# Expert blocks of a mixture-of-experts stage that hold at most 64 tokens: both parts of the tokens in one matmul operand

## The chip, the cores and the metric

The kernel runs on one core of a Trainium2 chip. The metric is the device time of one execution in microseconds (us), lower is better. The kernel before took 2165.18 us (median of three runs, 2159.99 to 2166.26).

The engines are named as the profile names them: PE is TensorE, DVE VectorE, ACT ScalarE, POOL GpSimd and SP SyncE. [...]

## What is computed

The reference is one layer: a recurrent token mixer, and then a mixture of experts over 1024 tokens of width 1024. Only the second half of the expert part matters here. Each token goes to 8 of 64 experts. The 8192 assignments are sorted by expert and each expert's list is padded to blocks of 128 rows. Then for each block:

```python
def expert_block(acc, blk):
    toks, wr, e = blk
    xb = x_pad[toks]                                   # 128 rows gathered
    hid = jax.nn.silu(xb @ w1[e]) * (xb @ w3[e])       # "up": 1024 -> 256, twice
    return acc.at[toks].add((hid @ w2[e]) * wr[:, None].astype(xb.dtype)), None   # "down", scattered
```

The reference works in float32.

## The kernel before, in words

**Numbers in two parts.** [...] So each operand is split into a high part, which is the value cast to `F32R`, and a low part, which is the value less its high part. A product is then three matmuls into the same accumulator: high by high, high by low, low by high. The helper `mm3` (L1639 to L1642) issues these three passes; L1640, L1641 and L1642 are its lines.

**Routing.** One function (up to L1537) computes on the chip which expert each block has, which tokens it holds and where they go. VectorE does most of it. It leaves `gi` and `si` (rows to gather and to scatter, one column for each block), `beb` (the expert of each block) and `meta`, a row of integers: 128 experts, 128 flags that say whether a block's expert differs from that of the block two places before (the weights are kept in two sets, for even and odd blocks), and the number of blocks. The blocks are dealt out so that even positions go through the first half of the experts' list and odd positions through the second half. Places of a block without a token gather row 0 and scatter to spare rows.

**The block loop** is `moe` (L1540 on). Its order is written out by hand (`tc.manual_schedule`), each engine takes its instructions in that order, and the function `group` (L1692) holds it. For block b, in order:

- `gather(b + 2)`: POOL gathers 128 rows of the tokens (L1611), two buffers.
- `up(b)`: TensorE multiplies the transposed tokens (stationary, `xh` and `xl`) by the expert's first weights (moving, `wh` and `wl`, 512 columns for both up matrices), eight pieces of the depth with three passes each, into `pa`.
- `hid_split(b - 1)`: ScalarE and VectorE split the hidden values of the block before into `hh` and `hl`.
- `store(b - 2)`: ScalarE scales the result by the token's weight (L1687), POOL scatters it with addition (L1689).
- `split_l(b - 1, 2)`, `split_h(b + 1, 0)`, `split_l(b + 1, 0)`, `split_h(b + 1, 1)`: ScalarE casts a 1 MB piece of weights to its high part (L1598), VectorE takes the difference (L1604). Each expert has three pieces: 0 and 1 for up, 2 for down. They stand under `fresh`, a `tc.If` on the block's flag, so that they run only when the expert is new. After a difference, SP loads the same piece for the block two later (L1581), conditional on that block's flag.
- `act(b)`: Silu on ScalarE (L1655), and its product with the other half on VectorE, `hd` (L1656).
- `x_t(b + 1)`, `x_split(b + 1)`: TensorE transposes the gathered tokens of the next block into `pt` (L1621), ScalarE casts them to `xh` (L1631) and VectorE takes the difference `xl` (L1632), in two halves; a small instruction (L1636, `jk`) picks the token's weight.
- `split_h(b, 2)`, `split_l(b + 1, 1)`: the remaining pieces of weights.
- `down(b - 1)`: twelve matmuls into `py`, and `hid_t(b)`: TensorE transposes `hd` into `ph` (L1663).

`xh` and `xl` have one buffer each, `pa` and the weights two. The first 95 blocks (`NB0`) run always; the rest of the possible 128 stand in groups of three under a `tc.If` on the number of blocks (L1741), and all engines jump over them here. After the loop come the final sum and norm.

When a `tc.If` is not taken, the engine still has to raise its semaphore by what the skipped instructions would have raised. It does so with an event instruction that first waits until the engine's earlier instructions are done.

Of the kernel before, what the change touches and what calls it, by code (L numbers as in the profile page):

```python
# [21 lines left out]
DVE = mybir.EngineType.DVE  # L22

# [7 lines left out]
NB = 128  # L31
NB0 = T * 8 // P + 64 // 2 - 1
# [9 lines left out]
def tile_kernel(ctx: ExitStack, tc: tile.TileContext, A: dict, dbg=None):  # L42
# [919 lines left out]
    meta = rt.tile([1, 2 * NB + 1], I32, name="meta")  # L962
# [410 lines left out]
def dispatch(nc, tc, A, ident, ones, sc, gi, si, beb, iot, meta, h2d):  # L1373
    V, S, G, PE = nc.vector, nc.scalar, nc.gpsimd, nc.tensor
    with tc.tile_pool(name="ds", bufs=1, side="right", reuse_waits="tile") as q, \
# [91 lines left out]
        V.tensor_tensor(pst, pend, nbk, ALU.subtract)  # L1467
        V.tensor_scalar(pst, pst, float(P), 1.0, ALU.mult, ALU.add)
# [38 lines left out]
        pbe = qp.tile([P, NB], F32, name="pbe")  # L1507
        PE.matmul(pbe, ones, dg, start=True, stop=True)
        V.tensor_copy(beb, pbe)
        br_ = beb[0:1]  # L1510
# [8 lines left out]
        V.tensor_copy(meta[:, 2 * NB :], nb[0:1])  # L1519
# [20 lines left out]
def moe(nc, tc, A, ident, h2d, accs, gi, si, beb, iot, meta, later):  # L1540
    V, S, G, PE = nc.vector, nc.scalar, nc.gpsimd, nc.tensor
    with tc.tile_pool(name="mo", bufs=1, reuse_waits="tile") as q, tc.tile_pool(name="mop", bufs=1, space=PSUM, reuse_waits="tile") as qp:
# [41 lines left out]

        def fresh(b, eng):
# [38 lines left out]
        def x_split(b):  # L1624
            if b >= NB:
                return
            xh = rot(q, [P, D], F32R, "xh", 1)
            xl = rot(q, [P, D], F32R, "xl", 1)
            for hf in range(2):
                s = slice(hf * 512, hf * 512 + 512)  # L1630
                S.copy(xh[:, s], PX[b][hf])  # L1631
                V.tensor_tensor(xl[:, s], PX[b][hf], xh[:, s].bitcast(F32), ALU.subtract)  # L1632
            XT[b] = xh, xl

            jk = rot(q, [P, 64], F32, "jk", 2)
            V.scalar_tensor_tensor(jk, iot[:, :64], beb[:, b : b + 1], XG[b][:, D:], ALU.is_equal, ALU.mult,  # L1636
                                   accum_out=rw[:, b : b + 1])

        def mm3(out, lh, ll, rh, rl, start, stop):  # L1639
            PE.matmul(out, lh, rh, start=start, stop=False)  # L1640
            PE.matmul(out, lh, rl, start=False, stop=False)  # L1641
            PE.matmul(out, ll, rh, start=False, stop=stop)  # L1642

        def up(b):
            AA[b] = rot(qp, [P, 512], F32, "pa", 2)
            for k in range(KD):
                ws = slice((k % 4) * 512, (k % 4) * 512 + 512)
                ks = slice(k * P, k * P + P)
                mm3(AA[b], XT[b][0][:, ks], XT[b][1][:, ks], WH[b, k // 4][:, ws], WL[b, k // 4][:, ws],
                    k == 0, k == KD - 1)  # L1650
# [33 lines left out]
        def store(b):  # L1684
            if b in YP:
                y = rot(q, [P, D], F32, "y", 2)
                S.mul(y, YP.pop(b), rw[:, b : b + 1])  # L1687

                G.indirect_dma_start(accs[b % 2], IndirectOffsetOnAxis(ap=si[:, b : b + 1], axis=0), y, None,  # L1689
                                     compute_op=ALU.add)  # L1690

        def group(lo, hi):  # L1692
            split_h(lo, 0)
            split_l(lo, 0)
            x_t(lo)
            x_split(lo)
            split_h(lo, 1)
            split_l(lo, 1)
            for b in range(lo, hi):
# [23 lines left out]
                if b > lo:  # L1723
                    down(b - 1)
# [6 lines left out]
        with tc.manual_schedule():  # L1731
# [7 lines left out]
            nb = nc.values_load(meta[0:1, 2 * NB : 2 * NB + 1], min_val=0, max_val=NB,  # L1739
# [170 lines left out]
```

## Time and profile before

| | us |
|---|---|
| median of three runs | 2165.18 |
| the profiled execution | 2165.25 |
| its span, first to last instruction | 2163.5 |
| expert loop, first up product to last down product | 1184.8 to 2095.1 |
| PE busy | 2040.4 (94%), 10575 matmuls and as many weight loads |
| DVE busy | 1282.8 (59%) |
| ACT busy | 992.4 (46%) |
| POOL busy | 541.7 (25%) |
[...]

The expert loop fills the second half of the span. A matmul's row has a modelled end: the next one starts before it. The distance from start to start is what a matmul costs when nothing waits. "Idle before" is the engine's pause ahead of an instruction, with what ended it. A name with a small q (PEldq, ACTq) is the engine's sequencer: register loads, branches and event instructions, which do not count as busy.

### The profile page before, as it was taken

To read this page: it belongs to the slowest core of one execution; us is meant where nothing else is said; L and a number is where in the kernel's file an instruction comes from. 1 tells how busy PE (TensorE), PEld (TensorE's weight loads), DVE (VectorE), ACT (ScalarE), POOL (GpSimd) and SP (SyncE) were. 2 spreads that over 40 slices of the span, in tenths; PEclk is the share of its full clock that TensorE was granted. 3 is DMA by queue.
4 is the path that set the end of the run, shared out by engine and by line. 5 is a ranking of instruction groups with operands and counts; after the bars stand their busy time and mean duration, and the time that the engine had idled before them with its cause. 6 is when DMAs were issued, how large, how long until landed. Compare 5 with 4: busy or idle time off the path is not lost. (4 is left out here: it accounts for less than half of the span.)

```text
span 2163.5 us, 29638 instructions
## 1 busy us (share of the span) xinstructions
PE 2040.4 (94%) x10575; PEld 1658.1 (77%) x10575; DVE 1282.8 (59%) x2047; ACT 992.4 (46%) x1352; POOL 541.7 (25%) x395
## 2 busy tenths in 40 slices
PE   6799999999999999998999999999989999999983
PEld 2488888898777788876777888788878888787861
DVE  7854664645668543444577666666454657775726
ACT  4335554634533411113234566566454657765721
POOL 5510000000033000010101344444333434444421
PEclk8799999999999999998998999999999999999996
DMA  8250100101053443456435799899898899999969
GB/s 306 73 153 26 40 30 30 39 30 49 30 172 135 142 137 116 128 170 245 159 111 224 248 307 338 258 313 297 240 310 240 267 280 358 368 347 270 332 136 238
DMA packets 107800, 416.17 MB, mean 192 GB/s; under 512 B 15250, under 2 KB 22034, under 8 KB 87668
## 3 DMA queue, kind: packets, MB, share of 16 engines
q1 hardware_dynamic: 62688, 260.03, 34.1%
q0 software_dynamic: 35376, 135.65, 23.6%
q10 hardware_dynamic: 9572, 18.46, 2.4%
q8 instruction: 85, 1.39, 0.3%
q14 instruction: 79, 0.65, 0.1%
HBM read 465.44 MB, written 90.20 MB: 257 GB/s over the span
## 5 line engine op out<-in xcount | busy, mean ns | idle before, releaser
L1604 DVE TENSOR_TENSOR wl<-raw,wh 128x2048 fp32r<-128x2048 f32 x156 | 356.3, 2288 | 61.4 <-ACT wh L1598 61.4
L1598 ACT CAST wh<-raw 128x2048 fp32r<-128x2048 f32 x156 | 294.8, 1919 | 43.0 <-DMA raw<-in_wm_dram 42.9
L1640 PE MATMUL pa<-wh,xh 128*128 128x512 f32 x760 | 304.9, 401 | 0.2 <-ACT xh L1631 0.2
L1641 PE MATMUL pa<-wl,xh 128*128 128x512 f32 x760 | 298.2, 392 | 2.8 <-DVE wl L1604 2.8
L1642 PE MATMUL pa<-wh,xl 128*128 128x512 f32 x760 | 298.7, 393 | 0.1
L1611 POOL DMA_INDIRECT xg<-h2d,gi x97 | 164.3, 1694 | 480.1 <-issue 326.5
L81 PE MATMUL z<-xl,wH 128*128 128x512 f32 x672 | 271.3, 404 | 8.1 <-DVE xl L293 8.1
L80 PE MATMUL z<-hH,wH 128*128 128x512 f32 x672 | 269.2, 401 | 2.7 <-ACT hH L290 1.6
L82 PE MATMUL z<-hH,wL 128*128 128x512 f32 x672 | 267.8, 399 | 0.0
L1689 POOL DMA_INDIRECT acc<-y,si x95 | 214.7, 2261 | 90.1 <-ACT y L1687 47.7
L1641 PEld LDWEIGHTS pa<-wl,xh 128*128 128x128 f32 x760 | 143.5, 189 | 33.6 <-DVE wl L1604 6.5
L1642 PEld LDWEIGHTS pa<-wh,xl 128*128 128x128 f32 x760 | 143.0, 188 | 32.2 <-DVE xl L1632 2.4
L1640 PEld LDWEIGHTS pa<-wh,xh 128*128 128x128 f32 x760 | 143.2, 188 | 27.2 <-ACT xh L1631 0.5
L1640 PE MATMUL py<-wh,hh 128*128 128x512 f32 x380 | 156.8, 413 | 6.4 <-ACT y L1687 6.4
L81 PEld LDWEIGHTS z<-xl,wH 128*128 128x128 f32 x672 | 127.8, 190 | 35.2 <-DVE xl L293 11.8
L1641 PE MATMUL py<-wl,hh 128*128 128x512 f32 x380 | 149.1, 392 | 0.8 <-DVE wl L1604 0.8
L80 PEld LDWEIGHTS z<-hH,wH 128*128 128x128 f32 x672 | 127.7, 190 | 28.1 <-ACT hH L290 1.8
L1642 PE MATMUL py<-wh,hl 128*128 128x512 f32 x380 | 149.1, 392 | 0.0
L82 PEld LDWEIGHTS z<-hH,wL 128*128 128x128 f32 x672 | 128.1, 191 | 24.6 <-issue 0.7
L125 DVE TENSOR_TENSOR wL<-wraw,wH 128x1024 fp32r<-128x1024 f32 x56 | 73.4, 1318 | 121.9 <-ACT wH L120 121.7
L1656 DVE TENSOR_TENSOR hd<-sl,pa 128x256 f32<-128x256 f32 x95 | 40.0, 421 | 175.2 <-ACT sl L1655 175.2
L1632 DVE TENSOR_TENSOR xl<-pt,xh 128x512 fp32r<-128x512 f32 x190 | 122.4, 686 | 18.6 <-ACT xh L1631 18.1
(522 smaller groups left out, 3897.5 us busy)
## 6 DMA issues: line engine op xcount, KB each, us to landing
raw<-in_wm_dram SPq DMA_DIRECT2D x285, 1024.0 KB
wraw<-in_wz_dram SPq DMA_DIRECT2D x50, 512.0 KB
wk<-in_w_ada_dram SPq DMA_DIRECT2D x64, 256.0 KB
raw<-in_wm_dram POOLq DMA_DIRECT2D x6, 1024.0 KB, 7.7
acc<-x POOLq DMA_DIRECT2D x9, 512.0 KB, 5.8
xl<-in_xcT_dram SPq DMA_DIRECT2D x16, 256.0 KB
mgd<-ga POOLq DMA_DIRECT2D x16, 256.0 KB, 3.1
xr<-in_xc_dram SPq DMA_DIRECT2D x8, 512.0 KB
```

The costliest lines, as they stand in the source:

```text
L80: PE.matmul(out, lh, rh, start=start, stop=False)
L81: PE.matmul(out, lh, rl, start=False, stop=False)
L82: return PE.matmul(out, ll, rh, start=False, stop=stop)
L125: V.tensor_tensor(L, raw, H.bitcast(F32), ALU.subtract)
L1598: S.copy(WH[b, c], raw[b % 2][c])
L1604: V.tensor_tensor(WL[b, c], raw[b % 2][c], WH[b, c].bitcast(F32), ALU.subtract)
L1611: G.indirect_dma_start(XG[b], None, h2d, IndirectOffsetOnAxis(ap=gi[:, b : b + 1], axis=0))
L1632: V.tensor_tensor(xl[:, s], PX[b][hf], xh[:, s].bitcast(F32), ALU.subtract)
L1640: PE.matmul(out, lh, rh, start=start, stop=False)
L1641: PE.matmul(out, lh, rl, start=False, stop=False)
L1642: PE.matmul(out, ll, rh, start=False, stop=stop)
L1689: G.indirect_dma_start(accs[b % 2], IndirectOffsetOnAxis(ap=si[:, b : b + 1], axis=0), y, None, compute_op=ALU.add)
```

## The change

For a block with at most 64 tokens, the 128 columns of the stationary operand hold the high parts of 64 tokens and, beside them, the low parts of the same 64 tokens. Two passes, against the weights' high and low parts, then give two sets of rows of `pa`, and their sum is the result; it holds the product low by low too. The routing makes a flag for each block, `half`, which each engine loads into a register and branches on. Such blocks gather and scatter 64 rows. All other parts of a block (transposes, casts, down products) stay at 128 rows.

```diff
-    meta = rt.tile([1, 2 * NB + 1], I32, name="meta")
+    meta = rt.tile([1, 3 * NB + 1], I32, name="meta")
...
+        rend = q.tile([P, 64], F32, name="rend")
+        V.scalar_tensor_tensor(rend, pst, float(P), cnt, ALU.mult, ALU.add)
+        pst0 = q.tile([P, 64], F32, name="pst0")
+        V.tensor_copy(pst0, pst)
...
+        ls = q.tile([P, 64], F32, name="ls")
+        V.tensor_scalar(ls, pst0, pb, None, ALU.is_le)
+        V.tensor_tensor(ls, ls, le, ALU.subtract)
+        V.tensor_tensor(ls, ls, rend, ALU.mult)
+        rem = q.tile([P, 1], F32, name="rem")
+        V.tensor_reduce(rem, ls, AX.X, ALU.add)
+        V.scalar_tensor_tensor(rem, pb, -float(P), rem, ALU.mult, ALU.add)
+        V.tensor_scalar(rem, rem, P / 2 + 0.5, None, ALU.is_lt)
+        dgh = q.tile([P, P], F32, name="dgh", tag="dg")
+        V.tensor_scalar(dgh, ident, rem, None, ALU.mult)
+        PE.matmul(pbh, ones, dgh, start=True, stop=True)
...
+        V.tensor_copy(meta[:, 2 * NB : 3 * NB], pbh[0:1])
...
+        def half(b, eng):
+            if (b, eng, 0) not in flags:
+                flags[b, eng, 0] = nc.values_load(meta[0:1, 2 * NB + b : 2 * NB + b + 1], engines=[eng], ...)
+            return tc.If(flags[b, eng, 0] > 0)
...
             XG[b] = rot(q, [P, D + 64], F32, "xg", 2)
-            G.indirect_dma_start(XG[b], None, h2d, IndirectOffsetOnAxis(ap=gi[:, b : b + 1], axis=0))
+            if b < 2:
+                G.memset(XG[b][H2:], 0.0)
+            with half(b, POOL) as c:
+                G.indirect_dma_start(XG[b][:H2], None, h2d, IndirectOffsetOnAxis(ap=gi[:H2, b : b + 1], axis=0))
+            with c.Else():
+                G.indirect_dma_start(XG[b], None, h2d, IndirectOffsetOnAxis(ap=gi[:, b : b + 1], axis=0))
...
                 S.copy(xh[:, s], PX[b][hf])
-                V.tensor_tensor(xl[:, s], PX[b][hf], xh[:, s].bitcast(F32), ALU.subtract)
+            with half(b, DVE) as c:
+                for hf in range(2):
+                    rest(xh[:, hf * 512 : hf * 512 + 512], PX[b][hf])
+            with c.Else():
+                for hf in range(2):
+                    s = slice(hf * 512, hf * 512 + 512)
+                    V.tensor_tensor(xl[:, s], PX[b][hf], xh[:, s].bitcast(F32), ALU.subtract)
...
+        def rest(h, x):
+            v = h.rearrange("p (k t) -> p k t", t=P)
+            V.tensor_tensor(v[:, :, H2:], x.rearrange("p (k t) -> p k t", t=P)[:, :, :H2],
+                            v[:, :, :H2].bitcast(F32), ALU.subtract)
...
         def mm3(out, lh, ll, rh, rl, start, stop):
             PE.matmul(out, lh, rh, start=start, stop=False)
-            PE.matmul(out, lh, rl, start=False, stop=False)
-            PE.matmul(out, ll, rh, start=False, stop=stop)
+            PE.matmul(out, lh, rl, start=False, stop=stop and ll is None)
+            if ll is not None:
+                PE.matmul(out, ll, rh, start=False, stop=stop)
...
+            def products(xl):
+                for k in range(KD):
+                    ...
+                    mm3(AA[b], XT[b][0][:, ks], XT[b][1][:, ks] if xl else None, WH[b, k // 4][:, ws], WL[b, k // 4][:, ws],
+                        k == 0, k == KD - 1)
+            with half(b, TEN) as c:
+                products(False)
+            with c.Else():
+                products(True)
...
+            tu = rot(q, [H2, 512], F32, "tu", 1)
+            hv = [slice(i * 256, i * 256 + 256) for i in range(2)]
+            with half(b, ACT):
+                for v in hv:
+                    S.copy(tu[:, v], AA[b][H2:, v])
+            with half(b, DVE):
+                for v in hv:
+                    V.tensor_tensor(AA[b][:H2, v], AA[b][:H2, v], tu[:, v], ALU.add)
             S.activation(sl, AA[b][:, :256], AF.Silu)
...
+                with half(b, POOL) as c:
+                    G.indirect_dma_start(accs[b % 2], IndirectOffsetOnAxis(ap=si[:H2, b : b + 1], axis=0), y[:H2], None,
+                                         compute_op=ALU.add)
+                with c.Else():
+                    G.indirect_dma_start(accs[b % 2], IndirectOffsetOnAxis(ap=si[:, b : b + 1], axis=0), y, None,
+                                         compute_op=ALU.add)
```

`H2` is 64. `jk` has one buffer in place of two.

## Rows read from the trace of the kernel before

**Rows 1.** The page's groups: line, engine, operation, names, count | busy us, mean ns | idle.

```profile
L1598 ACT CAST wh<-raw 128x2048 fp32r<-128x2048 f32 x156 | 294.8, 1919 | 43.0 <-DMA raw<-in_wm_dram 42.9
L1642 PE MATMUL pa<-wh,xl 128*128 128x512 f32 x760 | 298.7, 393 | 0.1
L1611 POOL DMA_INDIRECT xg<-h2d,gi x97 | 164.3, 1694 | 480.1 <-issue 326.5
L1689 POOL DMA_INDIRECT acc<-y,si x95 | 214.7, 2261 | 90.1 <-ACT y L1687 47.7
```

**Rows 2.** Busy time by stretch of the expert loop; columns named in the rows.

```profile
core 0: us, PE busy (x) PEld busy (x) DVE busy (x) ACT busy (x) POOL busy (x), PEclk, DMA share, GB/s
...
1290.00:1390.00 100.00, 95.53 (x464) 77.32 (x463) 72.75 (x83) 68.08 (x72) 45.63 (x22) 1.00 0.97 315
1390.00:1490.00 100.00, 100.00 (x498) 83.38 (x496) 55.83 (x80) 55.34 (x67) 38.68 (x22) 1.00 0.93 289
...
sum 910.00, PE 893.77 PEld 738.11 DVE 566.71 ACT 548.57 POOL 373.75; mean PE 89.38 PEld 73.81 DVE 56.67 ACT 54.86 POOL 37.38
```

**Rows 3.** TensorE in order of time, one block: start us, us, what.

```profile
1646.74 0.48 PE L1640 MATMUL pa<-wh,xh 128*128 128x512 f32 x1
...
1652.07 0.39 PE L1642 MATMUL pa<-wh,xl 128*128 128x512 f32 x1
1652.30 1.03 PE L1621 MATMUL pt<-ident,xg 128*128 128x128 f32 x8
...
1656.05 0.48 PE L1640 MATMUL pa<-wh,xh 128*128 128x512 f32 x1
```

**Rows 4.** Instructions of one line (L1597): count, ns min/median/max, first and last start.

```profile
L1597 ACTq EVENT_SEMAPHORE  x129: 17/17/17, 1206.0 to 2083.6; - x129
```

**Rows 5.** The same for line L1640, weight loads and the sequencer.

```profile
L1640 PEld LDWEIGHTS pa<-wh,xh x760: 186/188/331, 1184.8 to 2086.6; 128*128 128x128 f32 x190
...
L1640 PEldq EVENT_SEMAPHORE  x1: 51/51/51, 1184.4 to 1184.4; - x1
```

**Rows 6.** VectorE in order of time, block with a new expert next.

```profile
1668.86 2.29 DVE L1604 TENSOR_TENSOR wl<-raw,wh 128x2048 fp32r<-128x2048 f32 x1 [2.39 <-ACT wh L1598]
1671.53 0.42 DVE L1656 TENSOR_TENSOR hd<-sl,pa 128x256 f32<-128x256 f32 x1 [0.38 <-ACT sl L1655]
1672.17 1.29 DVE L1632 TENSOR_TENSOR xl<-pt,xh 128x512 fp32r<-128x512 f32 x2 [0.22 <-ACT xh L1631]
```

**Rows 7.** TensorE in order of time, start of that block.

```profile
1665.36 0.48 PE L1640 MATMUL pa<-wh,xh 128*128 128x512 f32 x1
```

**Rows 8.** ScalarE in order of time, the same block.

```profile
1666.92 3.72 ACT L1598 CAST wh<-raw 128x2048 fp32r<-128x2048 f32 x2
...
1671.55 1.08 ACT L1631 CAST xh<-pt 128x512 fp32r<-128x512 f32 x2
```

**Rows 9.** Instructions of line L1739, register loads after the loop.

```profile
L1739 PEldq TENSOR_LOAD <-meta x1: 483/483/483, 2092.1 to 2092.1; - x1
```

**Rows 10.** Instructions of line L1741, the branch over unused groups.

```profile
L1741 PEldq COMPARE_BRANCH  x1: 3746/3746/3746, 2092.7 to 2092.7; - x1
...
L1741 POOLq INC_SWDGE_SEM  x1: 1987/1987/1987, 2102.8 to 2102.8; - x1
```

**Rows 11.** TensorE in order of time, the last twelve down products.

```profile
2092.05 0.50 PE L1640 MATMUL py<-wh,hh 128*128 128x512 f32 x1 [1.48 <-ACT y L1687]
...
2094.68 0.39 PE L1642 MATMUL py<-wh,hl 128*128 128x512 f32 x1
```

**Rows 12.** VectorE in order of time, routing.

```profile
1142.60 0.22 DVE L1496 SCALAR_TENSOR_TENSOR bf<-pf,isb 128x64 f32<-128x64 f32 x1
```

**Rows 13.** DMA queues of the page: kind, packets, MB, share of 16 engines.

```profile
q8 instruction: 85, 1.39, 0.3%
q14 instruction: 79, 0.65, 0.1%
```

**Rows 14.** DMA issues by line: count, median us from issue to landing.

```profile
xg<-h2d,gi POOLq DMA_INDIRECT x97, 9.2
...
acc<-y,si POOLq DMA_INDIRECT x95, 11.5
```

More of the change, by code (lines that the diff above doesn't have):

```diff
@@ L22 @@
 DVE = mybir.EngineType.DVE
+TEN = mybir.EngineType.PE
 P = 128
@@ L31 @@
 NB = 128
+H2 = 64
 NB0 = T * 8 // P + 64 // 2 - 1
@@ L1518, in dispatch @@
         V.tensor_copy(meta[:, NB : 2 * NB], fl)
-        V.tensor_copy(meta[:, 2 * NB :], nb[0:1])
+        V.tensor_copy(meta[:, 2 * NB : 3 * NB], pbh[0:1])
+        V.tensor_copy(meta[:, 3 * NB :], nb[0:1])
         pl = qp.tile([P, NB], F32, name="pl")
@@ L1583, in moe @@
         flags = {}
+        def half(b, eng):
+            if (b, eng, 0) not in flags:
+                flags[b, eng, 0] = nc.values_load(meta[0:1, 2 * NB + b : 2 * NB + b + 1], engines=[eng], min_val=0,
+                                                  max_val=1, skip_runtime_bounds_check_because="made on chip within these bounds")
+            return tc.If(flags[b, eng, 0] > 0)
         def fresh(b, eng):
@@ L1631, in x_split @@
                 S.copy(xh[:, s], PX[b][hf])
-                V.tensor_tensor(xl[:, s], PX[b][hf], xh[:, s].bitcast(F32), ALU.subtract)
+            with half(b, DVE) as c:
[5 more added lines that the diff above has]
+                    V.tensor_tensor(xl[:, s], PX[b][hf], xh[:, s].bitcast(F32), ALU.subtract)
             XT[b] = xh, xl
-            jk = rot(q, [P, 64], F32, "jk", 2)
+            jk = rot(q, [P, 64], F32, "jk", 1)
             V.scalar_tensor_tensor(jk, iot[:, :64], beb[:, b : b + 1], XG[b][:, D:], ALU.is_equal, ALU.mult,
                                    accum_out=rw[:, b : b + 1])
+        def rest(h, x):
+            v = h.rearrange("p (k t) -> p k t", t=P)
+            V.tensor_tensor(v[:, :, H2:], x.rearrange("p (k t) -> p k t", t=P)[:, :, :H2],
+                            v[:, :, :H2].bitcast(F32), ALU.subtract)
         def mm3(out, lh, ll, rh, rl, start, stop):
             PE.matmul(out, lh, rh, start=start, stop=False)
-            PE.matmul(out, lh, rl, start=False, stop=False)
-            PE.matmul(out, ll, rh, start=False, stop=stop)
+            PE.matmul(out, lh, rl, start=False, stop=stop and ll is None)
+            if ll is not None:
+                PE.matmul(out, ll, rh, start=False, stop=stop)
         def up(b):
             AA[b] = rot(qp, [P, 512], F32, "pa", 2)
[L1646 to L1650, printed above, removed]
+            def products(xl):
+                for k in range(KD):
+                    ws = slice((k % 4) * 512, (k % 4) * 512 + 512)
+                    ks = slice(k * P, k * P + P)
+                    mm3(AA[b], XT[b][0][:, ks], XT[b][1][:, ks] if xl else None, WH[b, k // 4][:, ws], WL[b, k // 4][:, ws],
[4 more added lines that the diff above has]
+                products(True)
         def act(b):
@@ L1686, in store, with group @@
                 y = rot(q, [P, D], F32, "y", 2)
[L1687 to L1699, printed above, removed]
+                py = YP.pop(b)
+                S.mul(y, py, rw[:, b : b + 1])
+                with half(b, POOL) as c:
[4 more added lines that the diff above has]
+                                         compute_op=ALU.add)
+        def group(first_, hi):
+            split_h(first_, 0)
+            split_l(first_, 0)
+            x_t(first_)
+            x_split(first_)
+            split_h(first_, 1)
+            split_l(first_, 1)
+            for b in range(first_, hi):
                 last = b == hi - 1
@@ L1722, in group @@
                     split_l(b + 1, 1)
-                if b > lo:
+                if b > first_:
                     down(b - 1)
```

5 lines of the change are left out of this document (3 added, 2 removed).

## The prediction

> **What bounds the kernel now.** I read the page's groups first, then the table by stretch, then TensorE's order of time inside a block, then ScalarE and VectorE in the same block. The groups tell how often the loop runs: the up products are 760 of each of three passes, so 95 blocks of eight, and 156 casts `wh<-raw` are 52 experts of three pieces [rows 1]. That fits the reference's routing: worked out from its inputs (default seed), 52 experts get tokens, in 95 blocks, and 33 of the 95 hold at most 64 tokens. The table shows who is the limit: over the 910 us of the expert loop TensorE is busy 893.8, all of 1390 to 1490, and 4.5 us short in 1290 to 1390, where DMA's share is 0.97 and one new expert follows another [rows 2]. [...] So the loop is TensorE's, with small holes where weights come late.
>
> Inside a block nothing waits: up runs from 1646.74 to the transposes at 1652.30, and these, the down products and the hidden transposes lead to the next up at 1656.05 [rows 3]. A block takes 9.31 us; the 24 up products take 5.56 with the slower first one, 0.227 each (the last row of up and the next row are 0.23 apart).
>
> **The change part by part.**
>
> *Eight products fewer.* Eight times 0.227 is 1.81 us for each of 33 blocks: 60 us at most. This is the whole gain on offer; the transposes, the down products and the hidden transposes stay at 128 rows.
>
> *The join of the short arm.* The two arms raise TensorE's semaphore by different amounts, so the short one must add the rest after its own last product is done. ScalarE shows the habit: its skipped casts, three in each of 93 blocks less 150 done (156 without the first two blocks' six), are 129, and there are 129 event instructions [rows 4]. For TensorE the trace has no join between products. From below it costs nothing (the last product's increment could carry the difference). From above: the tail of a product past the next one's start, 0.39 less 0.23, and what lies between an event instruction and the weight load behind it, from 1184.4 to 1184.8 [rows 3, 5], together some 0.55. I take 0.5, by these rows: 1.3 us is left of 1.81.
>
> *The sum of the two parts, and its own chain.* Before Silu, ScalarE now copies two pieces of 64x256 and VectorE adds two. The nearest row is `hd`, as wide, at 0.42 [rows 6]. Two copies that overlap a little take some 0.7 (an estimate; at most 0.84), and the last add ends 0.45 after the last copy: 1.15 us longer to Silu. Whether that matters depends on the next block.
>
> Next block of an old expert (16 blocks, by the routing, and the last block): up ends at +3.7, Silu is done at +5.4, `hd` at +5.9, the two `xl` at about +7.2. TensorE, with join, transposes and down products, wants the next up at 9.31 - 1.81 + 0.5 = 8.0. All is hidden. 17 times 1.3 is 22 us.
>
> Next block of a new expert (16 blocks): ScalarE first casts that expert's first two pieces. In the block that starts at 1665.36 [rows 7] these run 1666.92 to 1670.64, that is to +5.3, and VectorE's `wl` ends at 1671.15, +5.8 [rows 6, 8]. Up at 3.7 is no help there: copies to +6.0, adds to +6.7, Silu +7.1, `xh` (1.08) +8.2, the second `xl` +9.1, and the next up now waits for both `xl`, as either arm of the split may have written `xh`. So the next block starts at +9.1, not +9.31; where it is itself a half block (5 of 16) the two differences of 64 rows are shorter and it is +8.7. That is 11 times 0.2 and 5 times 0.6: 5 us. Bounds: nothing to lose or gain beyond -0.5 each (-8) and 1.3 each (+21).
>
> *Branches.* Each block adds one register load and a branch on TensorE, ScalarE, VectorE and GpSimd. TensorE's one load in the trace took 0.48, its branch came 0.6 after the load's start [rows 9, 10]. The load ran at 2092.11, while the twelve down products of 2092.05 to 2094.68 were still to be done [rows 11]: its sequencer is at least 2.5 us ahead of its array. So I cost it at nothing; after a short arm's join that lead is rebuilt during the down products. Uncovered it would be 0.6 a block. On ScalarE and VectorE the branch and the join of the skipped copies come while they wait for TensorE; nothing in the 62 full blocks, where the later Silu (it waits for VectorE's join, after `wl` at +5.8) still leaves `xl` at +8.5 against 9.31.
>
> *Blocks where weights are late.* The loop's idle is 910 - 893.8 = 16 us [rows 2]. Fewer gathered and scattered rows free DMA there, which gives back nothing to 4.5 us, the hole of 1290 to 1390. But an up that waits for the second `xl` loses 0.65 (half of the pair's 1.29 [rows 6]) in each block that weights hold up, some eight (an estimate: 16 us at about 2 a hole): 5 us. Faster blocks before them also reach late weights sooner. I take -3 us (a loss), bounds -8 and +4.5.
>
> *GpSimd.* Gather and scatter cost it 1.69 + 2.26 = 3.95 us a block [rows 1]; it has 5.3 free. Added are the load and, if each arm's transfer has a semaphore of its own, a correction for the arm not taken. The only such row took 1.99 [rows 10]. Two of them make 8.4 with a load as long as TensorE's: still below 9.31. Nothing, as long as it fits.
>
> *Routing.* Some ten small VectorE instructions like `bf`, 0.22 each (a little over half of that from start to start, estimated, as they overlap) [rows 12], stand in a stretch in which VectorE has no pause: 1.4 us, bounds 0 (the shared expert's products fill TensorE) and 2.2.
>
> *Sum.* 22 + 5 - 3 - 1.4 = 23 us off the profiled execution's 2165.25 (span 2163.5, the rest around it): 2142 us. That execution lies on the median shown, 2165.18.
>
> [...] Short jumps cost no extra code loading in this trace: with 129 skipped casts on ScalarE alone [rows 4], one instruction queue brought 0.65 MB in 79 pages for all its engines; and another's 85 pages of 1.39 MB are TensorE's 21150 instructions once, 66 bytes each [rows 13]. The one long jump kept TensorE's sequencer 3.75 us [rows 10]. [...]
>
> **The rivals.**
> 1. *More is kept*: no join on TensorE, ScalarE's chain shorter than I add it, DMA's relief real. 17 times 1.81, 16 times 0.6, +3: 43 us, 2122. For it: the last product's increment may carry the difference. Against: ScalarE is busy to +5.3 whatever up does.
> 2. *TensorE leaves its queue at each branch*: 0.6 in 62 full blocks and 17 short ones is 47 us, 2142 + 47 = 2189, slower; half of it would be 2166. Against: the load's row with twelve products behind it.
> 3. *GpSimd becomes the loop's bound*: it decides when a correction costs more than (9.31 - 3.95 - 0.48) / 2 = 2.4 us. At 3.0, a wait for an old transfer before each 1.99, a full block takes 10.4, 62 times 1.1 is 68 us, and the half blocks lose their gain against some 8.5 (33 times 0.8 is 26 less): 2165 + 68 - 26 = 2207, slower. For it: transfers take 9.2 and 11.5 us to land [rows 14], and four semaphores a block in place of two come round sooner. Against: a block's room.
> [...]
> 5. *It hardly takes effect* (the flag is set for few blocks, or the gathers wait as before and weights set the pace): 2166, the same.
>
> **How the numbers follow.** Forecast 0.58, its own range 2128 to 2156; rival 1 0.16; 2 0.08, of which half near 2166; 3 0.08; 4 0.04; 5 0.06. What a measurement of this kernel can tell from no change is about 0.3%, 6.5 us. Faster: 0.56 + 0.16, so 0.72; the same: 0.02 of the forecast, 0.06 of rival 5, 0.04 of rival 2, so 0.12; slower 0.16. The range 2116 to 2172 takes in the forecast, most of rival 1, rival 5 and the mild half of rival 2.
>
> **What would show it.** `pa` third pass 496 times, the others 760. TensorE's time from an up's first product to the transposes 5.6 in full blocks, 3.7 plus the join in short ones. Blocks with an old expert behind them at about 8.0, with a new expert at 8.7 to 9.1, full ones at 9.31. Wrong is the prediction if full blocks stretch beyond 9.5 without late weights (rivals 2 to 4: the wait then names TensorE's queue, or `xg`), or if short blocks before a new expert reach 8.0.

## The result, and the profile after

The changed kernel takes 2142.8 us (median of four, 2141.1 to 2144.0) beside 2163.6 for the kernel before: ratio 0.9904, interval [0.9886, 0.9923], some 21 us faster. The profiled execution has a span of 2140.0 us against 2163.5. Forecast were 2142 us and a range of 2116 to 2172.

The page after: the lines that answer to [rows 1] and [rows 13], with the two busiest groups of the loop.

```profile
q0 software_dynamic: 31088, 117.53, 21.2%
...
q8 instruction: 99, 1.62, 0.3%
q14 instruction: 103, 0.84, 0.1%
...
L1633 DVE TENSOR_TENSOR wl<-raw,wh 128x2048 fp32r<-128x2048 f32 x156 | 355.8, 2285 | 42.8 <-ACT wh L1627 39.2
L1686 PE MATMUL pa<-wh,xh 128*128 128x512 f32 x760 | 310.5, 409 | 15.4 <-DVE xl L1672 8.7
L1627 ACT CAST wh<-raw 128x2048 fp32r<-128x2048 f32 x156 | 295.1, 1922 | 26.1 <-DMA raw<-in_wm_dram 25.9
...
L1689 PE MATMUL pa<-wh,xl 128*128 128x512 f32 x496 | 195.8, 395 | 0.0
L1645 POOL DMA_INDIRECT xg<-h2d,gi x63 | 113.9, 1809 | 299.0 <-DVE jk L1676 139.8
...
L1756 POOL DMA_INDIRECT acc<-y,si x62 | 150.7, 2430 | 46.2 <-ACT y L1750 20.5
```

The third pass runs 496 times, 62 blocks of eight, so 33 blocks take the short arm. The first pass of up (L1686) now has 15.4 us of idle time ahead of it, 8.7 of it put down to `xl`. ScalarE waits less for weights than before (25.9 us, 42.9 in [rows 1]).

A short block before an old expert, TensorE in order of time (block 30, the kernel after):

```profile
1466.10 0.48 PE L1686 MATMUL pa<-wh,xh 128*128 128x512 f32 x1
...
1469.61 0.39 PE L1687 MATMUL pa<-wl,xh 128*128 128x512 f32 x1
1469.85 1.03 PE L1655 MATMUL pt<-ident,xg 128*128 128x128 f32 x8
...
1473.46 0.38 PE L1725 MATMUL ph<-ident,hd 128*128 128x128 f32 x2
1473.59 0.48 PE L1686 MATMUL pa<-wh,xh 128*128 128x512 f32 x1
```

7.49 us from up to up, where [rows 3] show 9.31: 1.82 less, which is the eight products. Between the last up product (1469.61) and the transposes there is no wait for a join; in 31 of the 32 short blocks that another block follows the two starts are 0.23 to 0.24 apart.

A short block before a new expert is another matter (block 53, the kernel after; first TensorE, then ScalarE, then VectorE):

```profile
1679.82 0.47 PE L1686 MATMUL pa<-wh,xh 128*128 128x512 f32 x1
...
1683.34 0.39 PE L1687 MATMUL pa<-wl,xh 128*128 128x512 f32 x1
...
1686.95 0.39 PE L1689 MATMUL py<-wh,hl 128*128 128x512 f32 x1
1688.47 0.44 PE L1725 MATMUL ph<-ident,hd 128*128 128x128 f32 x2 [1.13 <-DVE hd L1718]
1689.51 0.47 PE L1686 MATMUL pa<-wh,xh 128*128 128x512 f32 x1 [0.60 <-ACT hh L1731]
```

```profile
1680.87 0.39 ACT L1731 CAST hh<-ph 128x256 fp32r<-128x256 f32 x1
1681.13 1.15 ACT L1750 ACTIVATE y<-py,rw 128x1024 f32<-128x1024 f32 x1
1682.13 3.75 ACT L1627 CAST wh<-raw 128x2048 fp32r<-128x2048 f32 x2
1685.91 0.64 ACT L1713 COPY tu<-pa 64x256 f32<-64x256 f32 x2
1687.58 0.38 ACT L1717 ACTIVATE sl<-pa 128x256 f32<-128x256 f32 x1 [1.03 <-DVE pa L1716]
1687.86 1.07 ACT L1665 CAST xh<-pt 128x512 fp32r<-128x512 f32 x2
```

```profile
1684.11 2.29 DVE L1633 TENSOR_TENSOR wl<-raw,wh 128x2048 fp32r<-128x2048 f32 x1 [0.20 <-ACT wh L1627]
1686.58 0.89 DVE L1716 TENSOR_TENSOR pa<-pa,tu 64x256 f32<-64x256 f32 x2 [0.18 <-ACT tu L1713]
1687.99 0.42 DVE L1718 TENSOR_TENSOR hd<-sl,pa 128x256 f32<-128x256 f32 x1 [0.53 <-ACT sl L1717]
1688.67 1.29 DVE L1672 TENSOR_TENSOR xl<-pt,xh 128x512 fp32r<-128x512 f32 x2 [0.26 <-ACT xh L1665]
```

The up products are done at 1683.6, but ScalarE casts the next expert's pieces until 1685.88, and only then starts the copies of the join. VectorE's `wl` ends at 1686.40, at about the same place. Then copies, additions, Silu, `xh` and `xl` follow one another, and the next up starts 9.69 us after this one. The bracket names `hh`; but what the next up waits for in all 16 such blocks is the first of the two `xl` (0.69 from 1688.67, so 1689.36): TensorE starts 0.14 to 0.26 after its end. In the kernel before the first up product needed no `xl`. In the kernel before the same block reads thus on ScalarE and VectorE:

```profile
1694.84 3.73 ACT L1598 CAST wh<-raw 128x2048 fp32r<-128x2048 f32 x2
1699.03 0.39 ACT L1655 ACTIVATE sl<-pa 128x256 f32<-128x256 f32 x1 [0.47 <-PE pa L1642]
```

It began at 1693.28. Its Silu came 5.75 after the start, that of the kernel after 7.76. The idle time ahead of the earlier Silu is put down to the up products: there ScalarE was done with the copies in time.

By the class of the block, from first up product to first up product, the sums of the two profiled executions are:

| | before | after | difference |
|---|---|---|---|
| up to the first up product | 1184.79 | 1185.22 | +0.4 |
| 16 short blocks, old expert next | 149.53 | 127.95 | -21.6 |
| 16 short blocks, new expert next | 155.19 | 157.08 | +1.9 |
| 62 full blocks | 592.40 | 594.68 | +2.3 |
| from the last block's up (short) to the end | 81.62 | 75.11 | -6.5 |

They add up to the span's 23.5 us. So the blocks before an old expert gave most of what TensorE saved, and those before a new one, taken together, nothing. These 16 fall in two: in the kernel before 12 of them take 9.32 us on the mean, and four, in which the weights of one new expert after another are late (blocks 17, 18, 78 and 79; in the kernel before block 78 still took 9.31), 10.85. After, the 12 take 9.17 and the four 11.77.

### The profile page after: what moved, and what is told of

It reads as the page before. It is cut to its first block, busy times and chain, and to the rows that moved or that the text cites. A ratio compares the mean times of both kernels' runs of the same rounds, so it can differ in the third digit from the quotient of the medians.

```text
span 2140.0 us, 30952 instructions
## 1 busy us (share of the span) xinstructions
PE 1994.5 (93%) x10313; PEld 1609.4 (75%) x10313; DVE 1298.0 (61%) x2123; ACT 1004.7 (47%) x1418; POOL 544.9 (25%) x397
## 5 line engine op out<-in xcount | busy, mean ns | idle before, releaser
L1686 PE MATMUL pa<-wh,xh 128*128 128x512 f32 x760 | 310.5, 409 | 15.4 <-DVE xl L1672 8.7
L1627 ACT CAST wh<-raw 128x2048 fp32r<-128x2048 f32 x156 | 295.1, 1922 | 26.1 <-DMA raw<-in_wm_dram 25.9
L1689 PE MATMUL pa<-wh,xl 128*128 128x512 f32 x496 | 195.8, 395 | 0.0
L1645 POOL DMA_INDIRECT xg<-h2d,gi x63 | 113.9, 1809 | 299.0 <-DVE jk L1676 139.8
L1686 PEld LDWEIGHTS pa<-wh,xh 128*128 128x128 f32 x760 | 146.3, 193 | 50.8 <-ACT xh L1665 7.6
L1756 POOL DMA_INDIRECT acc<-y,si x62 | 150.7, 2430 | 46.2 <-ACT y L1750 20.5
L1686 PE MATMUL py<-wh,hh 128*128 128x512 f32 x380 | 156.9, 413 | 4.6 <-ACT y L1750 4.6
L84 PEld LDWEIGHTS z<-hH,wL 128*128 128x128 f32 x672 | 128.0, 190 | 24.5 <-issue 0.7
L122 ACT CAST wH<-wraw 128x1024 fp32r<-128x1024 f32 x56 | 58.8, 1050 | 148.6 <-PE z L83 66.3
L1717 ACT ACTIVATE sl<-pa 128x256 f32<-128x256 f32 x95 | 36.5, 384 | 180.7 <-PE pa L1689 112.7
```

Source lines behind the costliest of these rows:

```text
L84: return PE.matmul(out, ll, rh, start=False, stop=stop)
L122: S.copy(H, raw)
L1627: S.copy(WH[b, c], raw[b % 2][c])
```

## The experiments

Ratios are to the kernel before on the same chip. Medians of the same kernel differ by several us from one set of executions to another (2159.0 to 2163.6 for the kernel before), so I read the ratios, and inside the loop the traces' starts. These recur: the kernel before and the kernel with branches but no gain (*branch_only*) agree within 0.7 us in each class of the table above, and within 1.4 us in each of the two groups of the new-expert class. Each kernel has one trace. Five of them (old_next, old_split, order, half_load_before, half_wh) are of executions 7 to 10 us below their kernel's median, and part of that lies ahead of the loop: their first up product comes at 1176.4 to 1181.6, that of the others at 1182.4 to 1188.2. So differences of a few us between loops are not shown by two traces alone. Means over the blocks, us after the block's first up product; "12" and "4" are the blocks before a new expert with weights in time and with late ones:

| kernel | ratio | old next: next up | 12: second weight copy ends | 12: Silu starts | 12: next up | 4: next up | first to last up | of it at half the full clock |
|---|---|---|---|---|---|---|---|---|
| before | 1 | 9.35 | 5.29 | 5.97 | 9.32 | 10.85 | 897.1 | 10.2 |
| branch_only | 1.0014 | 9.37 | 5.30 | 6.04 | 9.43 | 10.60 | 897.3 | 6.8 |
| rows_only | 0.9953 | 9.35 | 5.28 | 6.05 | 9.40 | 9.31 | 886.0 | 10.2 |
| up_only | 0.9948 | 7.88 | 5.71 | 7.40 | 9.25 | 12.21 | 882.7 | 30.5 |
| after | 0.9904 | 8.00 | 5.59 | 7.30 | 9.17 | 11.77 | 879.7 | 30.7 |
| old_next | 0.9892 | 7.97 | 5.66 | 6.26 | 9.17 | 11.01 | 872.7 | 10.2 |
| old_split | 0.9882 | 7.99 | 5.34 | 6.16 | 9.29 | 10.68 | 871.2 | 6.5 |
| no_sum | 0.9770 | 7.60 | 5.33 | 5.24 | 7.50 | 11.22 | 849.1 | 20.5 |
| order | 0.9978 | 8.27 | - | 7.59 | 9.50 | 11.48 | 892.0 | 17.1 |
| half_load_before | 0.9944 | 9.35 | 5.28 | 5.97 | 9.32 | 9.31 | 877.7 | 0 |
| half_load | 0.9861 | 7.95 | 5.54 | 7.26 | 9.22 | 10.36 | 871.6 | 17.1 |
| half_wl | 0.9879 | 7.75 | 5.64 | 7.24 | 9.10 | 11.92 | 873.8 | 30.7 |
| half_wh | 0.9865 | 7.87 | 3.72 | 6.37 | 8.24 | 12.10 | 862.4 | 20.5 |

(The copy's mean leaves out block 0, whose copies lie further back; a recorded start can lie a little ahead of the end of the instruction before it, as 5.24 beside 5.33 in *no_sum*.)

**branch_only: the branches without their gain.**

```diff
-                products(False)
+                products(True)
-                    rest(xh[:, hf * 512 : hf * 512 + 512], PX[b][hf])
+                    V.tensor_tensor(xl[:, s], PX[b][hf], xh[:, s].bitcast(F32), ALU.subtract)
-                G.indirect_dma_start(XG[b][:H2], ..., gi[:H2, b : b + 1] ...)
+                G.indirect_dma_start(XG[b], ..., gi[:, b : b + 1] ...)
```

(the scatter likewise; the join is gone, and with it ScalarE's branch and VectorE's second one)

> All the branches of the change on TensorE, VectorE (around the low parts) and GpSimd stay, but both arms do the whole work: 24 products, both low parts full, 128 rows; the sums and ScalarE's branch are left out. Theory A (branches are read ahead of their work and cost TensorE nothing, beyond 0.4 us in the routing): 2163 to 2166 us. Rival 2 of the prediction (TensorE leaves its queue at a branch): 2190 us or more. [...]

Measured: 1.0014 [0.9999, 1.0028]; the loop is 0.2 us longer. Theory A holds for the branches that this kernel has. TensorE's branches in the kernel after, from the view of their line (count, ns min/median/max):

```profile
L1700 PEldq COMPARE_BRANCH  x128: 65/204/352, 1180.6 to 2065.2; - x128
```

128 of them: one with a register load ahead of each of the loop's 95 blocks, and a second one, past the other arm, in each of the 33 short blocks. In branch_only the branch ends 2.0 us before the block's first up product (median), while the array still works on earlier products, as the prediction read off the one load in [rows 9]. It is not so everywhere: in ten blocks it ends only 0.06 us before, and in nine of these TensorE pauses, by 2.2 us in sum. The branches around the join are not in this kernel, so their price is not shown by it; the waits for `DVEq` under *order* below are theirs.

**up_only and rows_only: the two halves of the change.** The first gathers and scatters 128 rows always; the second keeps the 64 rows and runs 24 products in one stream without a join.

```diff
 up_only
-            with half(b, POOL) as c: ... 64 rows
-            with c.Else(): ... 128 rows
+            G.indirect_dma_start(XG[b], None, h2d, ...)     # and the scatter
 rows_only
-            with half(b, TEN) as c:
-                products(False)
-            with c.Else():
-                products(True)
+            products(True)                                   # and xl full, no join
```

> The two-pass arm alone: every gather and scatter moves 128 rows again, on GpSimd without a branch. Theory A (the products carry most of the gain in blocks before an old expert, and before a new expert the block waits for ScalarE's weight copies, which wait for their DMA): the weights arrive later than in the changed kernel, since the 18 MB of rows are back on the same queues; some 16 blocks lose about 0.6 us more each, and the tail is as before (about 4 us): 2153 to 2158 us. Rival B (the rows are hidden inside the loop and only the tail profits): 2145 to 2149 us. Rival C (GpSimd's branches cost as much as the rows save): 2140 to 2143 us.

> 64 rows gathered and scattered in short blocks, but the up products stay 24 in one stream, with no branch on TensorE, ScalarE and VectorE and no sums. Theory A: the weights come sooner in the blocks in which ScalarE waited for them (42.9 us of idle time before the weight copies in the kernel before), and the tail is shorter: 2152 to 2158 us. Rival B (rows only matter in the tail): 2158 to 2161 us. Rival C (rows cost GpSimd as much as they save): 2163 to 2166 us.

Measured: 0.9948 [0.9921, 0.9976] and 0.9953 [0.9936, 0.9970]; their product is 0.9901, the change itself 0.9904. The medians are 2146.1 and 2151.0 us: the one lies where rival B put it, the other 1 us below theory A's range. By the ratios each half is worth some 10 us (up_only's median lies 15 us under that of the kernel before beside it). That up_only came out where rival B put it does not make rival B's reason right: it had the rows hidden inside the loop. In the loop *rows_only* gains 11.1 us with not one product less: ScalarE waits 23.9 us for weights where it waited 42.9 [rows 1], the four blocks with late weights go from 10.85 to 9.31 each, 6.2 us, and the full blocks give 6.0. *up_only* gains 23.4 in the 16 blocks before an old expert and loses 4.7 in the 16 before a new one and 4.4 in the full ones. The weight copy's row in *rows_only*:

```profile
L1627 ACT CAST wh<-raw 128x2048 fp32r<-128x2048 f32 x156 | 294.4, 1917 | 24.0 <-DMA raw<-in_wm_dram 23.9
```

**old_next: the arm only where an old expert follows.** The flag is 2 there, 1 in the other short blocks.

```diff
+        V.tensor_scalar(fl, fl, 0.0, 1.0, ALU.is_equal, ALU.add)
+        V.tensor_tensor(meta[:, 2 * NB : 3 * NB - 1], pbh[0:1, : NB - 1], fl[:, 1:], ALU.mult)
-            return tc.If(flags[b, eng, 0] > 0)
+            return tc.If(flags[b, eng, 0] > (0 if eng == POOL else 1))
```

> The two-pass arm is taken only in short blocks whose next block has an old expert (17 of 33); the 16 others run 24 products and no sum. The 64 rows stay for all 33. [...] Rival B (these 16 blocks gain on the sum, by giving their time to the block after): 2146 to 2152 us. Rival D (the time in these blocks is set by the arrival of weights whatever TensorE does): 2141 to 2145 us.

Measured: 2135.6 us, 0.9892 [0.9872, 0.9912]. That lies in the 2134 to 2141 that I had expected if, in the other 16, the arm's sum and the shorter block are lost behind ScalarE's weight copies; but the interval overlaps that of the change, so that it is faster than the change is not shown. It is no slower: the 16 arms that it leaves out brought nothing. In its trace the 12 blocks take the same 9.17 with 24 products and no join, the four 11.01 instead of 11.77, and 10.2 us of the loop run at half the full clock instead of 30.7. But this execution is the fastest of its eight, with a mean granted clock of 0.978 where six of them had 0.965 to 0.974: the clock's part is not shown by it.

**no_sum: without the join.** The low part's 64 rows are computed and not added, so the output lacks that part.

```diff
-            with half(b, ACT):
-                for v in hv:
-                    S.copy(tu[:, v], AA[b][H2:, v])
-            with half(b, DVE):
-                for v in hv:
-                    V.tensor_tensor(AA[b][:H2, v], AA[b][:H2, v], tu[:, v], ALU.add)
```

> The changed kernel without the join: the low part's rows are not copied and not added to the products of short blocks (ScalarE's two copies and VectorE's two additions are left out); the arm itself stays. Theory A (in the 16 blocks before a new expert the four instructions stand between the late weight copy and Silu, 1.67 us in block 78): 16 times 1.2 to 1.7 us less, 2116 to 2126 us, and nothing in the blocks before an old expert. Rival D (the arrival of weights sets these blocks): 2139 to 2144 us.

Measured: 2112.5 us, 0.9770 [0.9746, 0.9793], below both theories' ranges. Inside the loop the join costs 20 us in the 12 blocks before a new expert (9.17 to 7.50 each), 2.2 in the four, and also 6.4 in the 16 others (128.0 to 121.6), where theory A had said there would be nothing: four instructions, nearly 30 us. Block 53 there, ScalarE and TensorE:

```profile
1668.55 3.73 ACT L1627 CAST wh<-raw 128x2048 fp32r<-128x2048 f32 x2
1672.15 0.41 ACT L1709 ACTIVATE sl<-pa 128x256 f32<-128x256 f32 x1
```

```profile
1666.99 0.48 PE L1686 MATMUL pa<-wh,xh 128*128 128x512 f32 x1
...
1674.35 0.38 PE L1717 MATMUL ph<-ident,hd 128*128 128x128 f32 x2
1674.48 0.48 PE L1686 MATMUL pa<-wh,xh 128*128 128x512 f32 x1
```

Silu follows the weight copies at once, and the block takes TensorE's 7.49 us. In the 12 blocks the first `xl`, which the next up needs, ends at 7.00 on the mean; in the kernel after it ends at 9.02, and the next up starts at 9.17. In the kernel before it ended at 7.72, and TensorE came to the next up at 9.32.

**half_load, on both kernels: is it the transfers?** Each later weight transfer brings half its columns; the rest stays from earlier blocks, so the result is not that of the layer.

```diff
-                nc.sync.dma_start(raw[b % 2][c], src, cond=f)
+                nc.sync.dma_start(raw[b % 2][c][:, :1024], src[:, :1024], cond=f)
```

> The changed kernel; from the third block on each weight transfer brings 1024 of its 2048 columns (the other half stays from earlier blocks), so that weights arrive in about half the time; all arithmetic is as before. Theory A (late weights ahead of ScalarE's queue take the gain in blocks before a new expert): 2105 to 2120 us, and these 16 blocks fall from 157 us in sum to 135 to 145 us. Rival F (ScalarE's own work, two copies of 1.92 us and the join, holds these blocks, not the transfers): 2137 to 2143 us, the 16 blocks at 152 us or more.

> The kernel before with the same halved weight transfers, as the control of the run beside it. Theory A: without late weights the blocks before a new expert fall to the 9.31 us that TensorE needs, 16 of them to 149 to 150 us in sum: 2145 to 2155 us, so that the change is worth 33 to 45 us there instead of 21. Rival F: 2155 to 2162 us, and the change is worth 20 to 24 us there too.

Measured: 2132.8 (0.9861 [0.9838, 0.9883]) and 2148.6 us (0.9944 [0.9922, 0.9966]): 15.8 us apart, neither the 33 to 45 of theory A nor the 20 to 24 of F. ScalarE's wait for weights is nearly gone:

```profile
L1627 ACT CAST wh<-raw 128x2048 fp32r<-128x2048 f32 x155 | 292.1, 1926 | 6.5 <-DMA raw<-in_wm_dram 6.5
```

and the 16 blocks take 152.1 us, as rival F said, while the time lies below F's range. The four blocks profit, 11.77 to 10.36; the 12 do not, 9.17 and 9.22. So late transfers hold four of the 16, and not the others: as an account of the whole class, theory A's transfers fall.

**half_wl and half_wh: which engine's queue?** Low parts, or copies, of half the columns; the other half stays from earlier blocks.

```diff
 half_wl
-                    V.tensor_tensor(WL[b, c], raw[b % 2][c], WH[b, c].bitcast(F32), ALU.subtract)
+                    n = 2048 if b < 2 else 1024
+                    V.tensor_tensor(WL[b, c][:, :n], raw[b % 2][c][:, :n], WH[b, c][:, :n].bitcast(F32), ALU.subtract)
 half_wh
-                    S.copy(WH[b, c], raw[b % 2][c])
+                    n = 2048 if b < 2 else 1024
+                    S.copy(WH[b, c][:, :n], raw[b % 2][c][:, :n])
```

> The changed kernel; from the third block on VectorE computes only 1024 of the 2048 columns of each low weight part (the other half stays from earlier blocks), so each of the three costs about 1.2 us instead of 2.29. Transfers, ScalarE's copies, products and the join are as before. Theory G (VectorE's queue holds the blocks before a new expert: the join's additions stand behind a low weight part, Silu behind the additions, the token splits behind Silu): the 16 blocks fall from 157 us to 138 to 146 us, the full ones profit too: 2112 to 2128 us. Rival F (ScalarE's queue alone holds them): 2136 to 2143 us.

> The changed kernel; from the third block on ScalarE copies only 1024 of the 2048 columns of each weight part (the other half stays from earlier blocks), about 1.0 us instead of 1.92; all else is as before. Theory G (VectorE's queue holds): the low parts can begin earlier, a few us: 2132 to 2140 us. Rival F (ScalarE's queue holds): 16 blocks at 138 to 146 us, 2112 to 2128 us. Both engines in turn (a chain through the two): about as much from this run as from the one beside it, 2122 to 2134 us each.

Measured: half_wl 2134.9 us, 0.9879 [0.9844, 0.9913], the 16 blocks unchanged (156.9). Theory G, VectorE alone, falls; the time is 1 us below rival F's range. half_wh: 2129.7 us, 0.9865 [0.9831, 0.9899], in the range of both engines in turn (which half_wl just misses), the 16 blocks 147.3, just above F's 138 to 146; all of it is in the 12 (9.17 to 8.24), the four with late weights stay (12.10). So in the 12 it is ScalarE's queue that ends last. VectorE's is close behind: with the shorter copies the join's copies start at 4.27, but the first addition only at 5.38, since VectorE still has `wl` ahead of it, and 8.24 is left where TensorE needs 7.5.

**order: the second weight copy behind Silu and the token splits.**

```diff
-                    split_h(b + 1, 1)
                 act(b)
                     x_split(b + 1)
+                    split_h(b + 1, 1)
```

> The changed kernel, with ScalarE's second weight copy of the next block behind the activation and the two splits of the tokens instead of ahead of them. Theory A (in blocks before a new expert the join and Silu stand behind a weight copy that waits for its DMA, in one queue): the wait of the hidden transposes goes in those 16 blocks, the low weight parts come a little later: 2128 to 2137 us. Rival D (TensorE waits for the arrival of weights in any order): 2141 to 2145 us. Rival E (the second weight copy then is late for the next block's products): 2147 us or more.

Measured: 2157.0 us, 0.9978 [0.9965, 0.9992], worse than the change: rival E. The loop's ScalarE row names the wait for VectorE's queue, and TensorE's row the low weight parts (21.9 us; 1.6 in the changed kernel):

```profile
L1717 ACT ACTIVATE sl<-pa 128x256 f32<-128x256 f32 x93 | 35.8, 385 | 235.7 <-PE pa L1689 92.4 <-DVEq L1714 87.7 <-DVE pa L1716 44.3
```

```profile
L1687 PE MATMUL pa<-wl,xh 128*128 128x512 f32 x742 | 295.6, 398 | 22.1 <-DVE wl L1633 21.9
```

ScalarE could have started Silu early, but the additions, and in full blocks VectorE's passing of the join that is not taken (`DVEq`, L1714), stand behind `wl` (27.1 us of such waits in the changed kernel, 87.7 here).

**old_wl2: a low part on GpSimd**, on top of old_next.

```diff
-                with fresh(b, DVE):
-                    V.tensor_tensor(WL[b, c], raw[b % 2][c], WH[b, c].bitcast(F32), ALU.subtract)
+                eng, X = (POOL, G) if c == 2 else (DVE, V)
+                with fresh(b, eng):
+                    X.tensor_tensor(WL[b, c], raw[b % 2][c], WH[b, c].bitcast(F32), ALU.subtract)
```

> As the run with the arm taken only before an old expert (2135.6 us, 0.989 of the kernel before), and the low part of the third weight block is computed by GpSimd instead of VectorE. No run shows what GpSimd takes for it. Theory G: VectorE is relieved of 2.29 us in each of 52 blocks: 2118 to 2130 us. Rival H (GpSimd takes longer than 4 us for it, and gathers and scatters wait behind it): 2140 to 2165 us.

Measured: 2309.9 us, 1.069 [1.0656, 1.0723], far beyond rival H. GpSimd takes 5.15 us, and VectorE's own low parts rise from 2.29 to 3.40 us on the mean:

```profile
L1636 POOL TENSOR_TENSOR wl<-raw,wh 128x2048 fp32r<-128x2048 f32 x50 | 257.7, 5153 | 0.1
```

```profile
L1636 DVE TENSOR_TENSOR wl<-raw,wh 128x2048 fp32r<-128x2048 f32 x104 | 353.7, 3402 | 83.2 <-ACT wh L1629 83.1
```

That mean hides two kinds. Of VectorE's 104 pieces 80 take 2.29 us as before. The other 24 lie beside a piece of GpSimd's and take 5.76 to 7.92, as this one of each engine:

```profile
1677.53 5.12 POOL L1636 TENSOR_TENSOR wl<-raw,wh 128x2048 fp32r<-128x2048 f32 x1
```

```profile
1678.04 6.77 DVE L1636 TENSOR_TENSOR wl<-raw,wh 128x2048 fp32r<-128x2048 f32 x1 [2.39 <-ACT wh L1629]
```

GpSimd's ends at 1682.65 and VectorE's at 1684.81. In all 24 VectorE ends 2.16 us after GpSimd, which is nearly its own time: it gets going only when GpSimd is done. In the two other meetings VectorE kept its 2.29 and GpSimd took 6.49 and 6.01.

**old_split: Silu between the two additions**, on top of old_next.

```diff
             with half(b, DVE):
-                for v in hv:
-                    V.tensor_tensor(AA[b][:H2, v], AA[b][:H2, v], tu[:, v], ALU.add)
+                V.tensor_tensor(AA[b][:H2, hv[0]], AA[b][:H2, hv[0]], tu[:, hv[0]], ALU.add)
             S.activation(sl, AA[b][:, :256], AF.Silu)
+            with half(b, DVE):
+                V.tensor_tensor(AA[b][:H2, hv[1]], AA[b][:H2, hv[1]], tu[:, hv[1]], ALU.add)
```

> As the run with the arm taken only before an old expert (2135.6 us, 0.989 of the kernel before), and Silu stands between the join's two additions, so that it waits for the first half of the columns alone; one more branch on VectorE. Without any join the 16 blocks before an old expert took 121.6 us where the arm's took 127.5. Theory J (that difference is ScalarE waiting for the second addition, 0.45 us a block, since the token splits come behind Silu): 16 times 0.3 to 0.4 us less, 2128 to 2131 us, ratio 0.985 to 0.988. Rival K (the rest of the chain, copies and first addition, holds them): 2134 to 2137 us. Rival L (the branch costs more than it saves): 2138 us or more.

Measured: 2133.3 us, 0.9882 [0.9854, 0.9910], between the ranges of J and K and not told apart from old_next; the trace decides. In blocks before an old expert Silu starts at 5.30 instead of 5.79 and `xh` ends at 6.65 instead of 7.14, but the next up stays (7.99 and 7.97). In block 63 the second addition now starts at 5.63 instead of 5.13, `hd` at 6.16 and 6.10, the first `xl` at 6.86 and 6.80. Theory J falls: ScalarE is earlier and the block gains nothing. The time is nearer to rival K's; the chain that ends last there is VectorE's own, additions, `hd`, `xl`, not Silu. But the edit lengthened that chain too: in all 16 blocks the second addition starts 0.03 after Silu's end. What the blocks would gain if it did not wait there is not shown.

## Why the prediction came out

The total was right (23 us forecast; 23.5 in the profiled executions, 21 between the medians), the parts less so. The products before an old expert came as forecast. The rest is in good part luck: the sum had the class before a new expert 7 us too good, and the end, the full blocks and the stretch ahead of the loop together about as much too bad.

- *Eight products fewer, old expert next.* Forecast a start at 8.0 and about 1.3 us a block; measured 8.00 and 21.6 us in 16 blocks. Right in size, wrong in cause: there is no join of the arms on TensorE (the 7.49 of block 30), so the term of 0.5 for it was not there, and the missing 0.5 is mostly the wait for the first `xl` behind the additions (in 12 of the 16 the next up starts 0.14 to 0.15 after its end). I had called the sum's chain hidden in these blocks; no_sum says that it costs 6.4 us.
- *New expert next.* The mechanism was right: copies to +5.3, then join, Silu, `xh` and `xl`, and the next up at 9.1 or 8.7. In the 12 blocks with weights in time the copies end at 5.59 and the next up starts at 9.17; that is 1.8 us gained. (Two errors cancelled there: the up waits for the first `xl` only, not for both as I had it, and the join costs more than the 1.15 to Silu that I worked out. In the 12 blocks, block 0 left out, Silu starts 1.72 after the copies' end in the kernel after, and 0.11 ahead of their recorded end in no_sum.) Wrong was to read one block [rows 6 to 8] as all 16: four of them wait for weights, and there the join comes on top. They lose 3.7 us (43.4 to 47.1), so that the class loses 1.9 where 5 of gain were forecast. My step for late weights had such a loss, 0.65 for each of some eight blocks; these four alone lose 0.9 each.
- *Rows.* Weighed at nothing to 4.5 us, and the step as a whole at a loss of 3. rows_only shows some 10 us, about half of the whole gain. [rows 1] had the sign: 42.9 us of ScalarE's wait for weights, which I set beside TensorE's 16 us of idle time and so took for covered.
- *The end.* Behind the last up product 6.5 us went; the sum had only the last block's 1.3. The three kernels with neither half of the change have 80.9 to 81.6 us there, rows_only 77.3 and up_only 77.9, so each half brings part of it; but the kernels with both range from 70.4 to 77.4, and I leave the split open.
- *Branches, GpSimd.* Nothing forecast, nothing measured (branch_only, within 0.3%; it lacks the join's branches). No GpSimd correction exists in the loop. *Routing*: VectorE's stretch from `cnt` to the last copy into `meta` takes 9.46 us instead of 8.66, so 0.8 where 1.4 was forecast. What of it reaches the loop is not shown: the first up product comes 0.4 later in these two executions, but between the kernels it varies by 12 us.
- *Full blocks.* They lose 2.3 us; the sum had its loss of 3 in blocks with late weights, for another reason. Some of it is the clock, below.

Of the rivals, more kept (1) was half true: there is no join on TensorE. Without the join's four instructions on ScalarE and VectorE the time is 2112, so these kept it from coming true. Rivals 2 and 3 are refuted in this kernel by branch_only: the loop is 0.2 us longer with the branches. Rival 5 is refuted by the 33 short blocks. No row and no run shows a source for the 0.04 of rival 4; what they show in its place is that the changed kernel's two instruction queues bring 99 and 103 packets instead of 85 and 79 [rows 13], and that the loop of branch_only, with 128 branches on TensorE, is longer by no more than those 0.2 us.

The shortest account that the runs bear: before an old expert TensorE was the bound, and pays out 1.35 us of 1.81. Before a new expert with weights in time TensorE had 9.32, and ScalarE's and VectorE's chain to the first `xl`, weight copies and all, 7.7. Without the join the shorter block goes at 7.5; the join moves the chain's end to 9.0, and nearly the whole gain is lost. In four blocks the weights' transfer is later still. The 18 MB of rows less on the DMA queues are worth some 10 us more (0.9948 without them, 0.9904 with them); how much of that falls in the loop and how much behind it the traces leave open.

## What to carry to other kernels

Before pricing fewer products, add up each other engine's queue for the same block, in order, and over all blocks of a class, not one of them: a gain ends where the second queue ends. Here that end was not far off, at 7.7 of 9.3 us, and the change itself moved it. A join that is cheap by its four instructions costs what stands behind it in two in-order queues, here nearly 30 us in 32 blocks; ask what waits ahead of it as well. Idle time of a helper engine waiting for a transfer can be a sign that bytes matter, even when the main engine looks covered: here it was ScalarE's 42.9 us, and the rows were worth some 10.

## What the runs showed of the hardware

TensorE's holes had a second price here. After block 53's two waits (1.13 and 0.60 us) the granted clock fell to half the full one for 3.4 us (0.51 on the mean of the second stretch); the table of stretches of the kernel after (columns named in it):

```profile
core 0: us, PE busy (x) PEld busy (x) DVE busy (x) ACT busy (x) POOL busy (x), PEclk, DMA share, GB/s
1680.00:1690.00 10.00, 8.27 (x40) 6.48 (x40) 7.72 (x12) 8.83 (x12) 3.80 (x2) 1.00 1.02 361
1690.30:1693.70 3.40, 3.40 (x10) 2.66 (x9) 2.72 (x3) 3.40 (x3) 2.37 (x2) 0.51 0.92 257
1693.70:1700.00 6.30, 6.30 (x33) 5.31 (x32) 4.20 (x7) 3.33 (x5) 3.32 (x1) 1.00 0.94 307
```

Inside it products start 0.43 us apart, and 0.23 outside. Ten products took those 3.4 us, 0.227 each would be 2.3; block 54, a full one, is 1.6 us longer than before, and 1.1 of it is this. The loop has 30.7 us at half the full clock after and 10.2 before (the mean granted clock of the whole execution is 0.966 and 0.969), each time behind pauses of TensorE: in the kernel after single ones of 1.58 to 3.10 us, or two as here, while pauses of 1.32, 1.44 and 1.77 us had no such stretch behind them. With TensorE busy half of the difference is lost, at most 10 us (an estimate from 30.7, 10.2 and the distances of 0.43 and 0.23, not an experiment: old_next, which has 10.2, is not shown faster). Where holes were many, in old_wl2, it was 106 us.

VectorE and GpSimd did not share their work on low weight parts but took turns: where the two met in old_wl2, one of them was held up, 24 times VectorE (5.76 to 7.92 us where it takes 2.29), until GpSimd's piece was done, and twice GpSimd (6.49 and 6.01, where the mean of its 50 is 5.15). In the kernel before, each of the 129 event instructions in place of ScalarE's casts starts 0.03 to 0.56 us after the end of ScalarE's last work, and VectorE's 129 0.04 to 0.75 after that of VectorE. And TensorE's 128 branches, 0.20 us each (median), cost the loop nothing that could be measured (897.3 us in *branch_only* beside 897.1), a register load of about 0.31 us (median in the changed kernel) ahead of each block included.
